# Longer allowances in a list scheduler's table: transfer to use, and VectorE or ScalarE to a matmul

## The chip, the cores and the metric

The kernel runs on one core of a Trainium2 chip. Its time is device microseconds, from the runs of the whole program; lower is better. The core's engines each take their instructions in the order in which they were issued: TensorE (PE, with its weight loads PEld), VectorE (DVE), ScalarE (ACT), GpSimd (POOL), and SyncE (SP), which here issues all DMA transfers.

## The reference, cut to what matters

Two layers over 1024 tokens of width 1024. In each, a normed and modulated input goes through one wide projection, whose columns feed three branches; their gated outputs are joined, projected back and added to the input. A last norm ends it. Everything is fp32.

```python
for l in range(DEPTH):                                    # DEPTH = 2
    mod = c_act @ ada_w[l] + ada_b[l]
    shift, scale, gate = jnp.split(mod[:, None, :], 3, axis=-1)
    h = rms_norm(x, norm_w[l]) * (1.0 + scale) + shift
    (q_lat, kv_lat, k_pe, g_mla, z, xbc, dt_raw,
     r, k, v, w_lo, a_lo, g_rwkv) = split_cols(h @ w_in[l], IN_SPLIT_SIZES)
    y_mla = mla_branch(...) * jax.nn.silu(g_mla)          # chunk-causal attention, 4 heads
    y_ssd = ssd_branch(...)                               # state space, chunks of 64
    y_rwkv = rwkv7_branch(...) * jax.nn.silu(g_rwkv)      # delta-rule recurrence, 8 heads of 64
    x = x + gate * (jnp.concatenate([y_mla, y_ssd, y_rwkv], axis=-1) @ w_out[l])
return rms_norm(x, final_norm_w)
```

## The kernel before, in words

The tokens are taken in two halves of 512, so there are four stages i = 0 to 3 (layer 0 half 0, layer 0 half 1, layer 1 half 0, layer 1 half 1). Each stage has two parts.

- **dense(i)**: the wide projection. 37 output tiles of 128 columns, each 24 matmuls of 128x512 into one PSUM bank of the tag `mf` (two banks in all). A weight tile comes in by DMA as `wr`, is split into a high part `wh` (ScalarE) and a low part `wl` (VectorE), and multiplies the split input (`h` tiles): high by high, high by low, low by high, in the type fp32r. ScalarE copies a finished bank to a tile `ct`, which SP stores to DRAM as `U`. From stage 2 on, dense(i) begins with the output projection of the layer before (`outproj`, 288 matmuls). After stage 3 come two more output projections (one for each half); the last of them ends with `outproj_last`, 48 matmuls over the last rwkv pair and the last attention head.
- **consumers(i)**: the branches. `rwkv` takes four pairs of heads in turn: `rwkv_a1` and `rwkv_a2` prepare them, `rwkv_bx` transposes through one PSUM bank of the tag `ra` (`ps623` to `ps633` are its banks for pair 1 of stage 0), `tinv_a` solves a triangular system in small VectorE steps, `rwkv_mr` and `chain` run the recurrence over eight chunks. In `chain`, each chunk's matmuls (`bx` by `gg`, 128x64) need the state that ScalarE and VectorE made of the chunk before. `ssd` and `mla` follow at the next rank; the attention of a head ends in a matmul with `vs` into `ps` (`ps4617` in the very last one), which VectorE multiplies into `gt`; SP stores it to `yd`, from where `y_split` loads it (`ct`), and ScalarE and VectorE split it into `h` tiles for `outproj`.

None of these calls issues an instruction. They are recorded as `Op`s, and `Plan.order` then writes one order for all engines: a list scheduler that steps through modelled time. For each queue (S is ScalarE, V VectorE, G GpSimd, P TensorE, Q SyncE) it keeps the ops whose inputs are there at the modelled time, and takes the one of the best rank. Ranks come from `plan.ahead`: rwkv before ssd and mla, these before the dense matmuls, so that the dense matmuls fill TensorE when no branch is ready; weight loads, weight splits and bank copies rank ahead of all. The order is fixed when the program is built: on the chip an engine does not skip an instruction that waits.

The table `LATENCY` enters at every edge between two ops. A key is the producer's letter and the consumer's: `SP` is ScalarE to TensorE, `VP` VectorE to TensorE, `D` stands for a DMA on either side. It is added to the producer's modelled end when the consumer becomes ready, and it is also added in `seat` when a buffer or a PSUM bank is taken over from its last user:

```python
t = max([t] + [end + LATENCY[at + o.at] for at, (end, _) in slots[tag][0][1].items()])   # seat: a freed buffer
ready[j] = max(ready[j], end + LATENCY[o.at + ops[j].at])                                # order: an input
```

All instructions are recorded on one line, L396, where the ordered ops are issued; the profile is therefore read by tile names.

Of the kernel before, what the change touches and what calls it, by code (L numbers as in the profile page):

```python
# [55 lines left out]
SG = ()  # L56
# [14 lines left out]
SX, SV, SB = 0, 0, 0  # L71
# [15 lines left out]

LATENCY = {"SS": 143, "SD": 147, "SV": 142, "SP": 270, "SG": 170, "VS": 128, "VD": 122, "VV": 127, "VP": 256, "VG": 155,  # L90
           "PS": 197, "PV": 196, "PD": 220, "PG": 224, "PP": 3, "GS": 75, "GD": 67, "GV": 60, "GP": 135, "GG": 102,
           "DS": 1700, "DV": 1700, "DP": 1850, "DG": 1700, "DD": 1700}


DMA_SP = True
# [148 lines left out]
class Plan:  # L244
# [41 lines left out]
    def order(self):  # L286
# [12 lines left out]
        def seat(o):  # L299
            t = 0.0  # L300
            for name in o.tiles:
                x = tiles[name]
                if x["free"] is None:
                    tag = x["tag"]
                    n = len(slots[tag]) - (0 if name.startswith("leafl") else owed[tag])
                    if n <= name.startswith("leafh") or not name.startswith("leaf") and name not in line[tag][:n]:
                        parked[tag].append(o)
                        return None
                    t = max([t] + [end + LATENCY[at + o.at] for at, (end, _) in slots[tag][0][1].items()])
                else:  # L310
                    t = max([t] + [end + LATENCY[at + o.at] for at, (end, _) in x["free"].items()])
                if x["bank"]:
                    t = max([t] + [end + LATENCY[at + o.at] for at, (end, _) in x["ends"].items() if at != o.at])
            return t
# [10 lines left out]
        while turn < len(ops):  # L325
# [58 lines left out]
            for j in o.next:  # L384
                ready[j] = max(ready[j], end + LATENCY[o.at + ops[j].at])
                wait[j] -= 1
# [1367 lines left out]
```

## Time and profile before

| | |
|---|---|
| median of 3 runs | 1990.66 us (1990.63 to 1992.5) |
| profiled execution: its time | 1993.3 us |
| profiled execution: first to last instruction | 1991.4 us |
| TensorE (PE) busy | 1848.3 us, 93% |
| VectorE busy | 1615.6 us, 81% |
| ScalarE busy | 1211.8 us, 61% |
| DMA packets, share of the 16 engines | 58.5% |
| mean granted TensorE clock | 0.972 |

Times in the profile are microseconds from the span's first instruction; the time of the profiled execution is 1.9 us above its span and 2.6 us above the median. TensorE's busy time comes from matmuls whose ends are modelled and which overlap, so the idle time between them and the granted clock say more than the share.

### The profile page before, as it was taken

How to read it: one execution, taken by the hardware profiler on the slowest of the kernel's cores; microseconds unless marked ns; L12 is line 12 of the kernel's file. 1: busy time of each engine (PE TensorE's matmuls, PEld its weight loads, DVE VectorE, ACT ScalarE, POOL GpSimd, SP SyncE). 2: the span in 40 equal slices, each digit the busy share in tenths (PEclk: the TensorE clock that was granted, in tenths of full speed). 3: DMA queues.
4: the chain of work that ended last, by engine and by line, in shares of the span. 5: the costliest groups of instructions: out<-in, count | busy, mean ns of one | idle time of the engine just before them, and what ended most of it. 6: DMA issues, size and time to landing. Idle time of an engine off the chain costs nothing. (4 is left out here: it accounts for less than half of the span.)

```text
span 1991.4 us, 32320 instructions
## 1 busy us (share of the span) xinstructions
PE 1848.3 (93%) x10220; PEld 1450.4 (73%) x10220; DVE 1615.6 (81%) x4002; ACT 1211.8 (61%) x2520; POOL 202.9 (10%) x302
## 2 busy tenths in 40 slices
PE   5899978999999996999999999999999999999997
PEld 3677756777777774777787777787777877777775
DVE  7798886888987898887678887878787888778766
ACT  6555565666555665746656647666656657676653
POOL 2100010001010101011100010002011010000101
PEclk9999988999999997999999999999999999999998
DMA  7676655755666576753555475855457556663542
GB/s 243 212 192 172 184 169 151 216 159 171 182 155 178 162 218 185 239 160 119 159 141 161 136 209 164 253 157 159 119 150 169 146 172 183 204 200 104 167 145 93
DMA packets 273371, 341.31 MB, mean 171 GB/s; under 512 B 79153, under 2 KB 132017, under 8 KB 273201
## 3 DMA queue, kind: packets, MB, share of 16 engines
q1 hardware_dynamic: 273200, 339.25, 58.5%
q8 instruction: 81, 1.33, 0.3%
q14 instruction: 90, 0.73, 0.1%
HBM read 254.67 MB, written 84.47 MB: 170 GB/s over the span
## 5 line engine op out<-in xcount | busy, mean ns | idle before, releaser
L396 PE MATMUL ps<-h,wh 128*128 128x512 f32 x3136 | 1021.1, 409 | 41.7 <-ACT ct L396 23.3
L396 PEld LDWEIGHTS ps<-h,wh 128*128 128x128 f32 x3136 | 580.8, 191 | 179.9 <-ACT ct L396 36.1
L396 PE MATMUL ps<-h,wl 128*128 128x512 f32 x1568 | 590.2, 408 | 2.3 <-DVE wl L396 2.3
L396 PE MATMUL ps<-b,b 128*128 128x128 f32 (+4 forms) x1512 | 388.9, 359 | 11.8 <-ACT b L396 4.0
L396 ACT ACTIVATE wh<-wr 128x512 fp32r<-128x512 f32 (+1 forms) x398 | 245.6, 620 | 220.1 <-PE ps L396 178.4
L396 PEld LDWEIGHTS ps<-h,wl 128*128 128x128 f32 x1568 | 296.8, 191 | 61.5 <-issue 4.8
L396 DVE TENSOR_TENSOR wl<-wr,wh 128x512 fp32r<-128x512 f32 (+1 forms) x398 | 268.7, 680 | 81.6 <-ACT wh L396 64.0
L396 PEld LDWEIGHTS ps<-b,b 128*128 128x128 f32 (+1 forms) x1512 | 232.2, 183 | 75.5 <-ACT b L396 18.1
L396 ACT ACTIVATE b<-b 128x512 f32<-128x512 f32 (+3 forms) x222 | 137.3, 626 | 71.6 <-DVE b L396 24.8
L396 DVE TENSOR_TENSOR b<-b,b 128x512 fp32r<-128x512 f32 (+4 forms) x178 | 121.4, 688 | 33.1 <-ACT b L396 32.2
L396 ACT ACTIVATE b<-ps 128x512 f32<-128x512 f32 (+3 forms) x201 | 99.5, 509 | 68.2 <-PE ps L396 63.0
L396 DVE TENSOR_TENSOR tmp<-Q,rq 128x60 f32<-128x60 f32 (+24 forms) x496 | 106.6, 215 | 5.7
L396 DVE TENSOR_TENSOR rq<-rq,tmp 128x60 f32<-128x60 f32 (+24 forms) x496 | 105.6, 213 | 5.2
L396 PEld LDWEIGHTS ps<-bx,gg 128*128 128x128 f32 x512 | 77.6, 194 | 41.3 <-ACT bx L396 14.4
L396 ACT ACTIVATE ct<-ps 128x512 f32<-128x512 f32 x150 | 88.1, 590 | 29.5 <-DMA U<-ct 9.9
L396 PE MATMUL ps<-cst,b 128*128 128x128 f32 x452 | 81.6, 282 | 15.2 <-POOL b L396 14.8
L396 POOL COPY halo<-ct 128x3 f32<-128x3 f32 x84 | 32.7, 389 | 616.2 <-ACT ct L396 616.1
L396 PE MATMUL ps<-bx,gg 128*128 128x64 f32 x512 | 83.5, 273 | 12.6 <-ACT bx L396 7.1
L396 ACT ACTIVATE b<-ps,s,s 128x512 f32<-128x512 f32 (+2 forms) x96 | 64.1, 669 | 39.3 <-DVE s L396 33.6
L396 PEld LDWEIGHTS ps<-cst,b 128*128 128x128 f32 x452 | 58.8, 146 | 30.9 <-POOL b L396 14.8
L396 DVE SCALAR_TENSOR_TENSOR h<-ps,md,h 128x512 f32<-128x512 f32 x72 | 53.7, 748 | 26.6 <-PE ps L396 26.1
L396 PEld LDWEIGHTS ps<-gg,bk 128*128 128x128 f32 x512 | 65.0, 193 | 14.1 <-issue 5.9
(196 smaller groups left out, 2598.7 us busy)
## 6 DMA issues: line engine op xcount, KB each, us to landing
wr<-in_w_in_dram SPq DMA_DIRECT2D x282, 256.0 KB
U<-ct SPq DMA_DIRECT2D x84, 257.5 KB
wr<-in_w_out_dram SPq DMA_DIRECT2D x80, 256.0 KB
U<-ct SPq DMA_DIRECT2D x64, 256.0 KB
ct<-in_ada_dram SPq DMA_DIRECT2D x64, 256.0 KB
ri<-U SPq DMA_DIRECT2D x52, 257.5 KB
b<-accd SPq DMA_DIRECT2D x96, 128.0 KB
ct<-yd SPq DMA_DIRECT2D x48, 256.0 KB
```

Source lines behind the costliest of these rows:

```text
L396: o.fn(*o.args, **o.kw)
```

## The change

Seven entries of the table grow; no op is added or removed, and each engine has the same instructions as before.

```diff
-LATENCY = {"SS": 143, "SD": 147, "SV": 142, "SP": 270, "SG": 170, "VS": 128, "VD": 122, "VV": 127, "VP": 256, "VG": 155,
+LATENCY = {"SS": 143, "SD": 147, "SV": 142, "SP": 500, "SG": 170, "VS": 128, "VD": 122, "VV": 127, "VP": 500, "VG": 155,
            "PS": 197, "PV": 196, "PD": 220, "PG": 224, "PP": 3, "GS": 75, "GD": 67, "GV": 60, "GP": 135, "GG": 102,
-           "DS": 1700, "DV": 1700, "DP": 1850, "DG": 1700, "DD": 1700}
+           "DS": 2200, "DV": 2200, "DP": 2350, "DG": 2200, "DD": 2200}
```

ScalarE to TensorE gets 230 ns more, VectorE to TensorE 244 ns more, and a transfer to whatever uses its data or its buffer 500 ns more. The scheduler thus sees a matmul ready later after its ScalarE or VectorE producer, and puts other ready matmuls ahead of it. In program order, the last matmul of dense(0) moves from place 1419 to 1196 among TensorE's 8408 matmuls and transposes, that of dense(1) from 3019 to 2863; the last chunk of the rwkv recurrence moves from 2102 to 2301 in stage 0, and from 3806 to 3989 in stage 1. In stages 2 and 3 these four kinds of places differ by less than 60.

Three places in the order matter below. Rows are an instruction's output tile, its inputs, its output's size and, after an x, how many follow each other.

**Place 1, TensorE, `rwkv_bx` of pair 1 in stage 0.** `ps410`, `ps439` and `ps448` are banks of dense(0); `ps617` is the bank of a head sum just ahead of the transposes `ps623` and on. Before:

```order
L396 MATMUL ps410_517<-h2153_260,wl416_523 128x512
L396 MATMUL ps617_724<-leafh618_725,bones_r_107 2x512
L396 MATMUL ps617_724<-leafl619_726,bones_r_107 2x512
L396 MATMUL ps623_730<-cst_99,gg565_672 128x128 x4
L396 MATMUL ps624_731<-cst_99,gg565_672 128x128 x4
L396 MATMUL ps625_732<-cst_99,bk564_671 128x128 x4
L396 MATMUL ps626_733<-cst_99,bk564_671 128x128 x4
L396 MATMUL ps862_969<-cst_99,b2859_966 128x128 x4
L396 MATMUL ps628_735<-cst_99,rv543_650 128x128 x4
L396 MATMUL ps633_740<-gg630_737,bk629_736 128x128 x4
```

Now:

```order
L396 MATMUL ps617_724<-leafl619_726,bones_r_107 2x512
L396 MATMUL ps439_546<-h2128_235,wl445_552 128x512
L396 MATMUL ps448_555<-h262_169,wh450_557 128x512
L396 MATMUL ps439_546<-h2141_248,wh444_551 128x512
L396 MATMUL ps448_555<-h263_170,wh450_557 128x512
L396 MATMUL ps439_546<-h2142_249,wh444_551 128x512
L396 MATMUL ps448_555<-h262_169,wl451_558 128x512
L396 MATMUL ps623_730<-cst_99,gg565_672 128x128 x4
```

Before, the transposes stand one bank behind the other, and 17 rows stand between `ps410` and the next dense row (`ps420`); now dense rows stand between all of them.

**Place 2, TensorE, `chain` of pair 1 in stage 1, near the start of dense(2).** `ps1710` takes the recurrence's first four chunks; `ps1510` and `ps1519` are banks of dense(1). Before:

```order
L396 MATMUL ps1710_1817<-bx1680_1787,gg1618_1725 128x64
L396 MATMUL ps1510_1617<-h21145_1252,wh1512_1619 128x512
L396 MATMUL ps1510_1617<-h21144_1251,wl1513_1620 128x512
L396 MATMUL ps1510_1617<-h21146_1253,wh1512_1619 128x512
L396 MATMUL ps1510_1617<-h21147_1254,wh1512_1619 128x512
L396 MATMUL ps1510_1617<-h21146_1253,wl1513_1620 128x512
L396 MATMUL ps1510_1617<-h21148_1255,wh1515_1622 128x512
```

Now:

```order
L396 MATMUL ps1707_1814<-bx1619_1726,Ez0_102 128x128 x4
L396 MATMUL ps1729_1836<-wa1547_1654,lora490_597 128x512
L396 MATMUL ps1729_1836<-wa1548_1655,lora490_597 128x512
L396 MATMUL ps1708_1815<-bx1619_1726,Ez0_102 128x128 x4
L396 MATMUL ps1915_2022<-cst_99,b21912_2019 128x128 x4
L396 MATMUL ps1710_1817<-bx1680_1787,gg1618_1725 128x64 x5
L396 MATMUL ps1921_2028<-cst_99,b21919_2026 128x128 x4
L396 MATMUL ps1710_1817<-bx1680_1787,gg1618_1725 128x64 x3
L396 MATMUL ps1922_2029<-cst_99,s1920_2027 128x128 x4
L396 MATMUL ps1711_1818<-bx1680_1787,gg1618_1725 128x64 x2
```

Here it goes the other way: dense(1) is already used up, and the chunks of `chain` now stand one behind the other with no dense row between them.

**Place 3, SP, the last attention output.** `gt4614` is that output, `yd3917` its place in DRAM, `ct4931` its way back into `y_split`; the `wr` loads are weights of the last output projection. Before:

```order
L396 DMA yd3917_4024<-gt4614_4721 128x256
L396 DMA wr4904_5011<-in_w_out_dram 128x384
L396 DMA ct4931_5038<-yd3917_4024 128x512
L396 DMA wr4908_5015<-in_w_out_dram 128x384
L396 DMA wr4912_5019<-in_w_out_dram 128x384
L396 DMA wr4916_5023<-in_w_out_dram 128x384
L396 DMA wr4920_5027<-in_w_out_dram 128x384
L396 DMA wr4924_5031<-in_w_out_dram 128x384
L396 DMA wr4934_5041<-in_w_out_dram 128x2x128 x2
```

Now:

```order
L396 DMA wr4924_5031<-in_w_out_dram 128x384
L396 DMA wr4934_5041<-in_w_out_dram 128x2x128 x2
L396 DMA wr4939_5046<-in_w_out_dram 128x2x128 x2
L396 DMA wr4944_5051<-in_w_out_dram 128x2x128 x2
L396 DMA wr4949_5056<-in_w_out_dram 128x2x128 x2
L396 DMA yd3917_4024<-gt4614_4721 128x256
L396 DMA ct4931_5038<-yd3917_4024 128x512
L396 DMA out_0_dram<-h24801_4908 128x512
```

The store and the load back moved behind all weight loads. On TensorE, the last attention matmul (into `ps4617`) was followed by 108 matmuls of the output projection before the first that reads the split of `ct4931` (`h24932`); now 16 stand between the two.

## The prediction

> **What bounds the kernel now.** I read the page's table of engines first, then the clock by slices, the waits of TensorE (PE), the windows in which it idles, and last the timeline of the end.
>
> ```profile
> PE 1848.3 (93%) x10220; PEld 1450.4 (73%) x10220; DVE 1615.6 (81%) x4002; ACT 1211.8 (61%) x2520; POOL 202.9 (10%) x302
> PE   5899978999999996999999999999999999999997
> PEclk9999988999999997999999999999999999999998
> core 0: 1991.4 us, clock 0.972
> ```
>
> PE is busy 93% and the bound over most of the span; the slices where it is not (first, sixth, sixteenth, last) are also those where the clock drops. VectorE (DVE) is busy 81%, so it can become the bound for a stretch of tens of us. No instruction is added, so the change can only alter PE's idle time and its clock. That idle time, by what ended it:
>
> ```profile
> PE ps L396 <- ACT ct L396: 23.3, 14, 3.6
> PE ps L396 <- POOL b L396: 14.8, 1, 14.8
> PE ps L396 <- ACT h L396: 10.6, 10, 1.9
> PE ps L396 <- ACT bx L396: 9.4, 10, 3.7
> PE ps L396 <- DVE ac L396: 9.1, 1, 9.1
> PE ps L396 <- DVE bx L396: 7.1, 5, 1.9
> PE ps L396 <- DVE h L396: 5.4, 10, 1.2
> PE ps L396 <- ACT gg L396: 5.1, 9, 2.3
> PE ps L396 <- ACT b L396: 4.0, 10, 0.9
> PE ps L396 <- DVE b L396: 3.8, 5, 1.4
> PE ps L396 <- DMA b<-accd: 3.7, 1, 3.7
> ACT b L396 <- DMA b<-accd: 17.2, 9, 6.0
> ```
>
> The columns are us in total, times, longest. The 14.8 us for POOL is the start of the program, which no allowance shortens. PE waits for a DMA itself only once, 3.7 us; so the 500 ns more on transfers acts on PE only through what ACT and DVE do later. The eight rows on ACT (ct, h, bx, gg, b) and on DVE (bx, h, b) make 68.7 us in 73 waits, 0.94 us each. That is four times the 0.23 us that an edge gains: most of these waits come from a producer whose queue is late, and not from the hop that the table prices.
>
> Three places carry the sum. The first is the transposes of pair 1 in stage 0 (Place 1), here in windows of us, each engine's busy time and count, the clock, the share of DMA and its GB/s, and then in PE's timeline and ACT's waits in the first window:
>
> ```profile
> 285.00:316.00 31.00, 14.28 (x49) 9.65 (x50) 25.78 (x75) 15.80 (x31) 3.87 (x5) 0.59 0.24 75
> 316.00:322.00 6.00, 6.00 (x16) 4.70 (x17) 3.40 (x5) 0.97 (x2) 0.19 (x1) 0.55 0.77 215
> ...
> 288.71 1.11 PE L396 MATMUL ps<-cst,gg 128*128 128x128 f32 x4 [0.68 <-ACT rt L396]
> 295.69 1.12 PE L396 MATMUL ps<-cst,bk 128*128 128x128 f32 x4 [2.26 <-ACT gg L396]
> 298.45 1.12 PE L396 MATMUL ps<-cst,rv 128*128 128x128 f32 x4 [0.79 <-ACT gg L396]
> 308.62 1.11 PE L396 MATMUL ps<-cst,s 128*128 128x128 f32 x4 [3.87 <-POOL s L396]
> 315.82 1.22 PE L396 MATMUL ps<-h,wh 128*128 128x512 f32 x2 [2.56 <-ACT ct L396]
> 318.54 0.63 PE L396 MATMUL ps<-h,wh 128*128 128x512 f32 x1
> 318.97 0.63 PE L396 MATMUL ps<-b,b 128*128 128x512 f32 x1
> 321.71 0.40 PE L396 MATMUL ps<-h,wh 128*128 128x512 f32 x1
> 321.95 0.39 PE L396 MATMUL ps<-b,b 128*128 128x512 f32 x1
> ...
> ACT b L396 <- DVE b L396: 7.7, 2, 7.4
> ```
>
> In 31 us PE works 14.28 and idles 16.7, while DVE is busy 25.78. Each transpose waits for the step before it, no dense row stands between, and the next dense row waits in its turn for ACT's copy of a bank (`ct`), which ACT reaches late because it has stood 7.4 us on DVE. The clock is 0.59 and stays 0.55 for 6 us after: dense matmuls there start 0.43 us apart (318.54 to 318.97), and 0.24 us apart once it is back (321.71 to 321.95). Of the 20.3 us busy in both windows, at a mean clock of 0.58, full speed would have saved some 8 (20.3 x 0.42 = 8.5). So this one place costs 16.7 + 8, about 25 us.
>
> The second is the boundary between dense(1) and dense(2):
>
> ```profile
> 757.00:779.00 22.00, 9.78 (x27) 6.80 (x28) 20.16 (x59) 7.06 (x12) 4.13 (x5) 0.53 0.75 252
> 779.00:790.00 11.00, 7.53 (x31) 5.05 (x30) 8.05 (x14) 9.61 (x15) 0.00 (x0) 1.00 0.32 81
> 766.71 1.11 PE L396 MATMUL ps<-cst,ac 128*128 128x128 f32 x4 [9.14 <-DVE ac L396]
> ```
>
> DVE is busy 20.16 of 22 us, so it is the bound there; PE idles 12.2 and 3.5 us and runs its 9.78 at 0.53, some 20 us lost in all (12.2 + 3.5 + 9.78 x 0.47 = 20.3).
>
> The Trainium skill has a rule on this ("TensorE: Matmul & The Clock Gate", section "What's actually happening"): TensorE drops to half clock after an idle window of about 3.4 us and needs about as long busy to come back. The trace agrees, with 0.53 around a wait of 9.14 us.
>
> The third is the end, from the last attention matmul to the use of its split (Place 3; SPq is the issue on SP's queue):
>
> ```profile
> 1938.95 0.39 PE L396 MATMUL ps<-b,b 128*128 128x128 f32 x2
> 1939.92 0.38 SPq L396 DMA_DIRECT2D yd<-gt  x1
> 1943.52 0.42 SPq L396 DMA_DIRECT2D ct<-yd  x1
> 1944.27 18.62 SPq L396 DMA_DIRECT2D wr<-in_w_out_dram  x13
> 1947.34 0.62 ACT L396 ACTIVATE h<-ct 128x512 fp32r<-128x512 f32 x1
> 1948.62 1.29 DVE L396 SCALAR_TENSOR_TENSOR h<-ct,h 128x512 fp32r<-128x512 f32 x2
> 1964.31 0.39 PE L396 MATMUL ps<-h,wh 128*128 128x512 f32 x1
> 1964.77 0.62 PE L396 MATMUL ps<-h,wh 128*128 128x512 f32 x2
> ...
> 1950.00:1964.00 14.00, 14.00 (x62) 10.73 (x61) 8.56 (x14) 3.72 (x7) 0.00 (x0) 1.00 0.37 107
> ```
>
> The way round DRAM takes from 1939.34 to 1949.91, 10.6 us; PE computes the output projection meanwhile without a gap and needs the split only at 1964.77.
>
> **The change, term by term.**
>
> *Place 1, a gain.* In the new order dense rows stand between all transposes of this stretch, so the waits of 0.68 to 3.87 us have matmuls to fill them and the clock has no reason to fall. DVE's 25.78 us of work remain; they lie beside dense work instead of beside nothing. At best the whole 25 us go; at worst none, if dense rows themselves wait for ACT's copies behind the 7.4 us on DVE. I take -25: in the new order three and more dense rows, on two banks, stand between one transpose and the next.
>
> *What pays for it.* The matmuls used there are not there later: dense(0) and dense(1) end 223 and 156 places earlier, the recurrences of stages 0 and 1 180 to 200 places later. Hence Place 2: ten groups of `chain` matmuls (5, 3 and 2 in the rows shown) without a dense row between, each needing the state that ACT and DVE make of the one before. The trace of before has no such hop uncovered; the nearest rows are the uncovered transposes at 288.71 and 298.45, with 0.68 and 0.79 us for one hop. Ten of them make 7 us. The low end is 0 (branch matmuls between may cover them); the high end doubles a hop, since the state passes through two engines: 14. I take +7.
>
> *The boundary.* DVE's 20.16 busy us in 22 do not depend on where dense matmuls stand, and what is late there, `ac`, is DVE's own queue. I take it as unchanged, 0; it could lose half its 20 us if the new order brings DVE's work forward, or gain as much if still less dense work is left for it.
>
> *Place 3, a loss.* Of 108 rows between the last attention matmul and the first that needs its split, 16 are left: 16 x 0.23 = 3.7 us of cover (0.23 is 1964.31 to 1964.77 over two rows). The chain is 10.6 us as it was. A part of it, the 3.6 us from store to load, holds for the new order too, since the load needs the store's data; with one split of the two needed first the chain is 7 to 8.6 us (to ACT's end, 1947.96). The hole is then 3.3 (7 - 3.7) to 6.9 us (10.6 - 3.7). Behind it stand some 42 matmuls of 0.23, 10 us; if the clock falls, part of them runs at half speed, by the row of 0.55 over 6 us above 2.7 us more (6 x 0.45). I take 5 for the hole and 2 for the clock, +7, between 3 and 10. By the skill's rule above, a hole under 3.4 us leaves the clock alone and one of 5 to 7 can halve it; the sum would be 1972 with the clock kept and 1974 with it halved.
>
> *SP's queue.* The store and the load back now stand behind all 14 remaining `wr` loads. Before, 13 of these were issued from 1944.27 on over 18.62 us, 1.4 us each, as the splits released their buffers. In the new order the last attention matmul itself stands 92 rows (108 - 16), some 21 us, later among the projection's matmuls, so the loads have that time and are out when it ends: 0. Should some be late, each adds 1.4 us to the hole; three would use up its high end.
>
> *The ordinary waits.* Outside those places, an edge allowed 0.23 us more can shorten a wait by at most that: 73 x 0.23 = 17 us. Since the mean wait is four times the allowance, and what is late is the queue, I take a third, -6 (0 to -17).
>
> *The transfers.* The 17.2 us that ACT waits for `accd` in 9 waits fall by at most 9 x 0.5 = 4.5 us, on ACT, 61% busy; behind ACT stands a DVE or PE step that has other work. Taken as 0.
>
> Sum: 1991.4 - 25 + 7 + 7 - 6 = 1974.4 for the span. The profiled execution's time lies 1.9 above its span and 2.6 above the median of the three runs, so the median becomes 1974.4 + 1.9 - 2.6 = 1973.7. I forecast 1974 us, 0.8% faster; its own range, with the term ends -25 to -15, 0 to 14, 3 to 10 and -17 to 0, is about 1958 to 1990 (not all ends at once).
>
> **Rivals.**
>
> *Slower: DVE is the bound through all of stages 0 and 1, and PE's idle time only moves.* For it speaks DVE's 25.78 of 31 and 20.16 of 22 us in both holes: PE waits where DVE is full, and dense work spent early is missing at the next such place. Then the 25 us of Place 1 return at the boundary or at the chains (the dense matmuls moved, 223 places x 0.23 = 51 us, are more than enough to open such a hole), and Place 2's clock falls as well. Time: 1991 + 7 for the tail, + 7 for Place 2, nothing else gained, 2004; 1998 to 2008. It decides once the early gain keeps less than the 14 us that the tail and Place 2 cost. Against it: outside the holes DVE has 19% idle, and PE is 93% busy without it.
>
> *No change.* The waits are set by late producers, allowances of 0.23 us reorder without filling, and Place 1's gain stops at some 14 us against the same costs: 1988 to 1994, about 1990. Against it stands that the new order visibly has dense rows in Place 1.
>
> *A larger gain.* The ordinary waits fall by their full 17 us, as dense rows step in wherever a producer is late, and the boundary's 20 us halve since DVE's queue reaches it earlier: 1974 - 11 - 10 = 1953. For it: ACT's `ct`, the largest row (23.3 us), is a wait for a bank and so a scheduled edge. Against it: the longest waits are producers that are full, which no order of PE makes faster.
>
> **Chances.** Main forecast 0.50, larger gain 0.16, no change 0.11, slower 0.23. 0.2%, 4 us, is about what a measurement of this kernel can tell from no change; so faster 0.66, the same 0.11, slower 0.23. The range 1945 to 2006 takes in the larger gain's time with 8 us below it and the slower rival's 2004.
>
> **What would show it.** Place 1 right: around the transposes of pair 1 in stage 0, PE is 95% busy or more and the clock stays at 1.00; wrong: a window with the clock near 0.6 there, or PE waiting on `ct` for several us. Place 2 right: a dozen waits of 0.5 to 1 us on `bx` ahead of `chain`'s matmuls at the start of dense(2), no more than 14 us together; wrong: a window of 20 us and more with the clock near 0.5. Place 3 right: one wait of 3 to 7 us for `h` in the last 30 us, some 42 matmuls before the last; wrong: no such wait. The ordinary waits right: the same eight rows at some 60 us; at 50 or less the larger gain has happened. The prediction fails as a whole if the boundary's loss, which I left as it is, grows by more than 15 us, which a wait on DVE longer than 9.14 us with a second half-clock stretch beside it would show.

## The result, and the profile after

The changed kernel takes 1955.28 us (median, 1952.39 to 1962.57) beside 1991.18 for the kernel before: a ratio of 0.9825 with an interval of 0.9811 to 0.984, 36 us faster where 17 were forecast. The profiled execution has a span of 1951.8 us, 39.6 less than before: the two profiled executions lie some 4 us further apart than the medians (1953.6 and 1993.3 us). Its table of engines, slices and clock:

```profile
PE 1825.9 (94%) x10220; PEld 1460.7 (75%) x10220; DVE 1619.7 (83%) x4002; ACT 1205.9 (62%) x2520; POOL 204.4 (10%) x302
PE   5899997999999986989999999998999999999996
PEclk9999998999999986999999999999999999999997
core 0: 1951.8 us, clock 0.975
```

The weak sixth slice of before is strong now, the seventh (293 to 342 us) has become weak in its place, and slices 15 and 16, 683 to 781 us, show 8 and 6, where before had 9 and 6. PE's waits by releaser (us in total, times, longest):

```profile
PE ps L396 <- ACT h L396: 21.4, 13, 3.4
PE ps L396 <- DVE b L396: 11.2, 9, 3.3
PE ps L396 <- DVE bx L396: 9.0, 7, 2.2
PE ps L396 <- DVE h L396: 7.7, 11, 1.5
PE ps L396 <- ACT ct L396: 5.4, 8, 2.6
PE ps L396 <- ACT bx L396: 3.8, 5, 1.7
PE ps L396 <- ACT b L396: 3.5, 7, 0.8
PE ps L396 <- ACT gg L396: 3.0, 7, 1.4
```

The eight rows that made 68.7 us in 73 waits make 65.0 in 67. Read as a total they say that next to nothing happened. Over all rows on ACT and DVE PE's waits fall from 103.7 us in 116 waits to 87.1 in 94, and they have moved in time, which the windows tell. The program is cut below where PE has done 600 and 900 us of the same matmul work in both kernels (how that is counted follows); first the three windows of before, then of the change, with PE busy, PEld, DVE, ACT, POOL, clock, DMA share and GB/s:

```profile
15.00:732.00 717.00, 654.63 (x3599) 504.05 (x3599) 608.73 (x1539) 433.13 (x910) 68.66 (x117) 0.96 0.64 182
732.00:1073.00 341.00, 317.50 (x1687) 250.50 (x1686) 277.62 (x705) 207.33 (x423) 34.50 (x50) 0.96 0.56 166
1073.00:1974.00 901.00, 872.77 (x4924) 693.68 (x4923) 715.62 (x1734) 559.07 (x1165) 84.90 (x116) 0.99 0.56 164
```

```profile
15.00:683.00 668.00, 630.09 (x3492) 500.10 (x3492) 588.04 (x1491) 418.11 (x885) 70.93 (x120) 0.99 0.68 196
683.00:1051.00 368.00, 329.49 (x1797) 261.30 (x1795) 300.86 (x742) 222.57 (x454) 35.73 (x52) 0.93 0.53 154
1051.00:1934.00 883.00, 862.95 (x4920) 697.27 (x4920) 717.02 (x1747) 553.17 (x1158) 82.83 (x112) 0.99 0.57 167
```

The first part is 49 us shorter (idle 62.4 to 37.9, clock 0.96 to 0.99), the middle, which holds the boundary from dense(1) to dense(2), 27 us longer (clock 0.96 to 0.93), the last 18 us shorter.

For the finer picture each matmul is given the median distance to the next start that its tiles and shape have in the trace of before; the running sum is PE's work, 1740 us in every kernel, and time less work is what has been lost so far. The table is that loss, as a difference to the kernel before (whose time at each mark stands in the first row), from the profiled execution of each kernel. The rows below the first two belong to the experiments.

| PE work done, us | 180 | 240 | 300 | 480 | 600 | 720 | 900 | 1320 | 1680 | 1737 |
|---|---|---|---|---|---|---|---|---|---|---|
| before: time | 239 | 333 | 400 | 603 | 732 | 883 | 1073 | 1531 | 1914 | 1974 |
| the change | -12.6 | -42.1 | -31.9 | -49.5 | -49.3 | -28.9 | -22.7 | -34.5 | -46.0 | -39.8 |
| hops 500 alone | +2.6 | -11.3 | -12.0 | -22.9 | -24.8 | -29.1 | -25.4 | -34.9 | -33.2 | -34.8 |
| hops 380 alone | +4.1 | -25.5 | -23.2 | -36.8 | -13.6 | +8.9 | +6.4 | -0.8 | -3.9 | -6.2 |
| hops 250 alone | +5.8 | -6.7 | -7.8 | -19.2 | +3.0 | +0.5 | +6.7 | +10.3 | +1.1 | +3.4 |
| hops 800 with transfers | -3.7 | -31.5 | -25.5 | -44.7 | -28.4 | -38.8 | -40.6 | -52.8 | -53.8 | -31.3 |
| the change in stage 0 only | -13.3 | -44.5 | -33.1 | -48.5 | -27.3 | -0.6 | +0.1 | +1.9 | +4.6 | +3.0 |
| the change with hops 480 | -9.2 | -35.4 | -25.6 | -41.8 | -27.7 | -3.1 | -2.4 | -5.4 | -5.1 | -7.0 |
| old table from stage 3's branches on | -12.3 | -43.9 | -33.0 | -50.8 | -50.0 | -29.6 | -23.7 | -30.8 | -32.5 | -33.3 |
| old table in stage 3's attention | -12.9 | -44.4 | -34.4 | -52.2 | -52.7 | -32.2 | -25.5 | -34.4 | -41.6 | -44.4 |

Of the change's 39.8 us, 17.3 are less idle time of PE, 3.3 are less time lost to the clock (half of the busy time at a granted clock of 0.5), and 19.2 are less time counted as busy at full clock. The wait lists show the first of these three alone.

**Place 1.** The transposes of pair 1 in stage 0 in the changed kernel, two windows and PE's timeline (the bracket is the idle time ahead and what ended it):

```profile
274.00:304.00 30.00, 29.22 (x143) 23.53 (x142) 27.66 (x77) 19.63 (x40) 8.48 (x9) 1.00 0.63 190
304.00:330.00 26.00, 17.22 (x63) 12.67 (x62) 23.93 (x50) 14.30 (x23) 3.01 (x5) 0.80 0.62 195
...
293.56 0.60 PE L396 MATMUL ps<-cst,bk 128*128 128x128 f32 x4
301.15 1.13 PE L396 MATMUL ps<-gg,bk 128*128 128x128 f32 x8 [0.78 <-issue]
312.28 0.50 PE L396 MATMUL ps<-h,wh 128*128 128x512 f32 x1 [3.42 <-ACT h L396]
323.30 1.11 PE L396 MATMUL ps<-cst,b 128*128 128x128 f32 x4 [3.31 <-DVE b L396]
```

PE is busy 29.22 of 30 us at full clock, beside DVE's 27.66. Right behind it, dense(0) is used up and dense(1) waits for its split input `h`: 8.8 us idle in the second window, and a clock of 0.80.

**Place 2 and the boundary.** Three windows, and in the second the waits of `chain`'s matmuls, the longest wait of another branch and the first dense row (the sixth wait of `chain`, 0.40 us, stands in the last section):

```profile
676.00:692.00 16.00, 8.93 (x52) 6.95 (x53) 13.53 (x39) 7.76 (x18) 0.00 (x0) 0.81 0.80 226
730.00:764.00 34.00, 21.36 (x89) 16.48 (x89) 30.89 (x86) 18.64 (x34) 4.37 (x4) 0.71 0.37 116
764.00:796.00 32.00, 22.33 (x89) 15.26 (x89) 28.93 (x77) 18.83 (x37) 4.11 (x3) 0.83 0.42 130
...
738.78 1.12 PE L396 MATMUL ps<-bx,gg 128*128 128x64 f32 x4 [2.16 <-DVE bx L396]
743.84 0.69 PE L396 MATMUL ps<-bx,gg 128*128 128x64 f32 x2 [1.82 <-DVE bx L396]
747.20 1.12 PE L396 MATMUL ps<-cst,s 128*128 128x128 f32 x4 [2.67 <-POOL s L396]
748.82 1.20 PE L396 MATMUL ps<-h,wh 128*128 128x512 f32 x2
755.22 0.44 PE L396 MATMUL ps<-bx,gg 128*128 128x64 f32 x2 [0.42 <-DVE bx L396]
757.12 0.43 PE L396 MATMUL ps<-bx,gg 128*128 128x64 f32 x2 [1.46 <-DVE bx L396]
759.16 0.69 PE L396 MATMUL ps<-bx,gg 128*128 128x64 f32 x2 [1.60 <-DVE bx L396]
```

The second window loses 12.6 us idle and, at a clock of 0.71 on 21.36 busy us, 6 more. Six of its waits, of 0.40 to 2.16 us and 7.9 us together, are the chain's own on `bx`, five of them ended by DVE, which is busy 30.89 of the 34 us. The other 4.7 us idle are waits of the branches beside it, 2.67 us on POOL's `s` the longest. Only up to 748.82 is the chain without dense rows; from there on rows of the output projection stand between its matmuls again.

**Place 3.** The end, SP's queue, ACT and PE:

```profile
1896.83 18.21 SPq L396 DMA_DIRECT2D wr<-in_w_out_dram  x11
1915.09 0.59 SPq L396 DMA_DIRECT2D yd<-gt  x1
1917.70 0.33 SPq L396 DMA_DIRECT2D ct<-yd  x1
1920.33 0.63 ACT L396 ACTIVATE h<-ct 128x512 fp32r<-128x512 f32 x1 [3.24 <-DMA ct<-yd]
...
1917.71 0.73 PE L396 MATMUL ps<-h,wh 128*128 128x512 f32 x2 [0.62 <-DVE h L396]
1921.01 1.95 PE L396 MATMUL ps<-h,wh 128*128 128x512 f32 x4 [2.33 <-ACT h L396]
1924.23 1.22 PE L396 MATMUL ps<-h,wh 128*128 128x512 f32 x2 [0.42 <-DVE h L396]
```

The last weight load is issued until 1915.04 and the store at 1915.09, half a microsecond after `gt` was ready (1914.58), so the queue that the store was moved behind cost at most that, where nothing was forecast. The split comes after PE has run out: 3.4 us idle (0.62 + 2.33 + 0.42), and matmuls at half rate behind it (4 in 1.95 us). By equal work the change loses 6.2 us here (-46.0 to -39.8).

### The profile page after: what moved, and what is told of

It reads as the page before. It is cut to its first block, busy times and chain, and to the rows that moved or that the text cites. A ratio compares the mean times of both kernels' runs of the same rounds, so it can differ in the third digit from the quotient of the medians.

```text
span 1951.8 us, 32300 instructions
## 1 busy us (share of the span) xinstructions
PE 1825.9 (94%) x10220; PEld 1460.7 (75%) x10220; DVE 1619.7 (83%) x4002; ACT 1205.9 (62%) x2520; POOL 204.4 (10%) x302
## 5 line engine op out<-in xcount | busy, mean ns | idle before, releaser
L396 PE MATMUL ps<-b,b 128*128 128x512 f32 (+4 forms) x1512 | 384.6, 356 | 10.5 <-DVE b L396 6.3
L396 ACT ACTIVATE b<-b 128x512 f32<-128x512 f32 (+3 forms) x222 | 136.9, 625 | 62.1 <-DVE b L396 25.6
L396 PEld LDWEIGHTS ps<-bx,gg 128*128 128x128 f32 x512 | 76.8, 194 | 32.2 <-DVE bx L396 15.8
L396 POOL COPY halo<-ct 128x3 f32<-128x3 f32 x84 | 28.6, 340 | 621.9 <-ACT ct L396 594.2
L396 POOL TENSOR_TENSOR s<-s,nhalf 128x4 f32<-128x4 f32 (+1 forms) x34 | 54.0, 1591 | 258.1 <-DVE s L396 250.5
L396 DVE SCALAR_TENSOR_TENSOR h<-ps,md,h 128x512 f32<-128x512 f32 x72 | 53.5, 746 | 33.2 <-PE ps L396 32.7
L396 ACT ACTIVATE b<-ps,s,s 128x512 f32<-128x512 f32 (+2 forms) x96 | 63.9, 667 | 27.3 <-DVE s L396 24.3
```

Of the source, the lines that this page charges most:

```text
L396: o.fn(*o.args, **o.kw)
```

## The experiments

Each was timed against the kernel before on the same chip; the ratio and its interval are given. The chips differ from group to group, so kernels of different groups are compared by their ratios.

**Which entries carry it.** Two kernels change one part of the table, a third all of it by a tenth, and a fourth goes further.

```diff
+"SP": 500, "VP": 500                                # hops only
```


> Only ScalarE and VectorE to TensorE are raised to 500; the transfer entries stay as before. Theory A (the allowance for the hop puts ready matmuls ahead of each waiting one, so the ordinary waits shrink): nearly all of the gain is here, 1955 to 1965 us, and PE's waits for ACT's copies (ct, 23.3 us before) are at 10 us or less. Theory B (any change of the table reshuffles the order, and where clusters of unfilled waits fall is luck): anywhere from 1950 to 2005, no relation to what was raised. Theory C (the transfer entries carry it): 1985 to 1995.

1958.68 us, 0.9861 (0.984 to 0.9883): inside theory A's range, though PE's waits on `ct` fell to 13.2 us and not to 10.

```diff
+"DS": 2200, "DV": 2200, "DP": 2350, "DG": 2200, "DD": 2200   # transfers only
```


> Only the transfer entries are raised by 500; the hops to TensorE stay as before. Theory A: no gain from fewer waits, 1985 to 1995; the waits on ct stay at some 20 us. Theory B: anywhere from 1950 to 2005. Theory C: 1955 to 1965.

1990.39 us, 1.0017 (0.9999 to 1.0035): the transfers alone bring nothing. PE's waits on `ct` nevertheless fell, to 12.3 us in 15, so the expectation on `ct` was wrong: that row does not measure the gain.

```diff
+"SP": 293, "VP": 280, "DS": 1750, "DV": 1750, "DP": 1900, "DG": 1750, "DD": 1750
```


> Every entry is raised by a tenth of the change (293, 280, and 50 more for a transfer). The order is reshuffled, the allowance hardly differs. Theory A: a tenth of the gain, 1984 to 1991. Theory B: as far from before as the full change, 10 to 40 us either way. Theory C: as A.

1992.86 us, 1.003 (1.0019 to 1.0042): no gain, and 6 us slower than before on that chip (1986.79), which none of the three theories gave.

```diff
+"SP": 800, "VP": 800, "DS": 2200, "DV": 2200, "DP": 2350, "DG": 2200, "DD": 2200
```


> The hops to TensorE go to 800, the transfers as in the change. Theory A: the ordinary waits shrink further, but dense(0) and dense(1) are used up earlier still, and the boundary to dense(2) loses more: 1945 to 1965, with the waits outside 650 to 800 us under half of before. Theory B: no relation, 1950 to 2005.

1970.39 us, 0.9914 (0.988 to 0.9948). In the table it is 53.8 us ahead at 1680 and loses 22.5 at the end, where a single row is left between the last attention matmul and the use of its split. It misses theory A's range and its condition (outside 650 to 800 us PE waits 80.8 us on ACT and DVE, before 82.8). The transfers alone bring nothing so far; that the size of the hop decides does not follow, since theory B allows all of these times but that of the tenth.

**Inputs or buffers.** The hop enters at an input and where a bank or buffer is taken over; here only one of the two is raised.

```diff
+EDGE = dict(LATENCY, **{'SP': 500, 'VP': 500})
-                ready[j] = max(ready[j], end + LATENCY[o.at + ops[j].at])
+                ready[j] = max(ready[j], end + EDGE[o.at + ops[j].at])
```


> Hops of 500 only where a matmul's input comes from ScalarE or VectorE; taking over a bank or buffer keeps the old allowance, and so do the transfers. Theory A1 (PE's waits are for inputs of the branches, which now have dense rows ahead of them): most of the 28 us of the run with both uses, 1958 to 1968. Theory A2 (the gain is in the turnover of the dense banks, PE's waits on ct): 1980 to 1992, with ct at 20 us or more.

1980.88 us, 0.9965 (0.9948 to 0.9982).

```diff
+SEAT = dict(LATENCY, **{'SP': 500, 'VP': 500})      # for LATENCY in seat, three times
```


> The other half: hops of 500 only where a bank or buffer is taken over. Theory A1: 1980 to 1992. Theory A2: 1958 to 1968, with PE's waits on ct under 15 us.

1991.81 us, 1.0006 (0.9991 to 1.002). Together the two gave 28 us, apart 9 and nothing. Neither theory predicted that; the spread of the runs around 500 below is as large, so which use matters stays open.

**The tail, and 800 without it.** Operations recorded from stage 3's branches on are ordered by the old table.

```diff
+        plan.late = i == 3; consumers(i, U)         # late: LATENCY as before, else the change's table
```


> The changed kernel, but everything recorded from the branches of stage 3 on is ordered by the old table. Stages 0 to 2 have the order of the change, and 173 rows stand again between the last attention matmul and the first use of its split. If the tail's hole costs what the prediction said, 7 us (6 by the changed kernel's waits), its waits there go, and the time is 1948 to 1952 unless stage 3's own waits return (before had 10 us more there than the change): then 1952 to 1960.

1959.14 us, 0.9855 (0.9836 to 0.9874). Up to 900 us of work it runs like the change, and at 1320 it is 3.7 us behind it. The tail's loss is gone (-32.5 to -33.3), and from 1320 to 1680 it gains 1.7 where the change gains 11.5: with the same stages ahead of it, this part is 10 us slower by the old table. Both terms came out as expected.

> Hops of 800 in stages 0 to 2, transfers as before, the old table from the branches of stage 3 on; 155 rows of cover at the end. The run with 800 everywhere was 54 us ahead of before by equal PE work until the tail, and lost 22 there with one row of cover. Theory A: without that loss 1930 to 1950. Theory B (the order is luck, 800 no better than 500): 1950 to 1990.

The same switch with hops of 800 and the old transfers: 1970.89 us, 0.9907 (0.9875 to 0.9939). The tail's loss is gone too, but so are 33 us of the gain ahead of it (-20.8 at 1680). This contradicts theory A in its simple form. The transfers' entries differ as well between the two runs with 800, so the switch is not the only difference.

**The size.** Hops alone, with 77 rows or more of cover at the end.

```diff
+"SP": 100, "VP": 90
```


> The other direction: hops to TensorE of 100 and 90 instead of 270 and 256, transfers as before, 139 rows of cover at the end. Theory A (the allowance itself sets the waits): slower, 1995 to 2020, with more PE waits on ACT and DVE than the 73 of before. Theory B (the order is luck): 1960 to 2000 with no more waits.

2030.85 us, 1.0209 (1.0185 to 1.0234), 43 us slower; over all its rows PE waits 130 times on ACT and DVE, 119.8 us, beside 116 times and 103.7 us in the kernel before. The direction is theory A's; the loss is larger than its range.

```diff
+"SP": 380, "VP": 380
```


> Hops of 380, about half of the way, transfers as before; 97 rows of cover at the end (94 at 500). Theory A: between before and the 1958.7 of 500, 1965 to 1982. Theory B: unrelated, 1950 to 2000.

1988.37 us, 1.0004 (0.9991 to 1.0018), a miss for theory A. At 480 us of work it is 36.8 us ahead, at 720 it is 8.9 behind.

```diff
+"SP": 650, "VP": 650
```


> Hops of 650, transfers as before; 77 rows of cover at the end. Theory A, with dense matmuls that run out: 1950 to 1968, near 500. Theory B: unrelated, 1950 to 2000.

1975.18 us, 0.9928 (0.9903 to 0.9952), outside of what A gave as well.

**Does stage 0's gain last?**

```diff
+        plan.late = i > 0; U = dense(i, spread)
+        plan.late = i > 0; consumers(i, U)
```


> The change's table for everything recorded for stage 0 (dense(0) and its branches), the old one for the rest. By equal PE work the change was 49.5 us ahead of before at 480 us of work, gave 23 back at the boundary to dense(2), and won 19.5 in stages 2 and 3. Theory of the prediction (what dense work stage 0 uses early is missing at the boundary, whatever orders stage 1): 15 to 30 of the 49 are given back there, 1960 to 1980 in all. Rival (the boundary's loss comes from stage 1's own longer allowances): it keeps more than 40 of the 49, 1945 to 1955.

1991.39 us, 1.0013 (0.9991 to 1.0035). It is 48.5 us ahead at 480 us of work, as the change is, and level with before at 720: everything was given back, more than either theory said, 21 us of it between 480 and 600 us of work (until 705 us in this run) and 27 between 600 and 720 (until 882). Three of its windows there, and then the last of them in the change, where PE is busy without a gap:

```profile
650.00:700.00 50.00, 38.28 (x176) 30.05 (x175) 40.06 (x105) 29.81 (x65) 9.27 (x11) 0.92 0.60 188
750.00:800.00 50.00, 35.39 (x164) 25.97 (x164) 45.89 (x120) 24.05 (x47) 7.37 (x6) 0.88 0.28 93
800.00:850.00 50.00, 35.28 (x231) 28.46 (x229) 39.12 (x69) 26.76 (x51) 5.74 (x5) 0.72 0.54 163
```

```profile
800.00:850.00 50.00, 50.00 (x325) 42.37 (x324) 36.54 (x72) 28.62 (x60) 5.05 (x5) 1.00 0.71 222
```

So the loss does not need stage 1's own longer allowances, as the rival had it. But it is not bound to the change's stage 0 either: hops of 250 are 19.2 us ahead at 480 and 0.5 behind at 720, while hops of 500 alone go from 22.9 ahead to 29.1. An early gain is often given back there, not always, and what decides it is open.

**The size or the one order?** Three orders close to 500.

```diff
+"SP": 490, "VP": 490
```


> Hops of 490 instead of 500, transfers as before; 103 rows of cover at the end (94 at 500). If the size of the allowance decides: within 6 us of 500's 1958.7, 1952 to 1965. If the particular order decides: as far off as 380 and 650 are, 1965 to 1990.

1980.31 us, 0.9958 (0.9943 to 0.9973).

```diff
+"SP": 510, "VP": 510
```


> Hops of 510, transfers as before; only 22 rows of cover at the end, which costs some 5 us by itself. If the size decides: 1955 to 1970. If the order decides: 1950 to 1990, and by equal PE work before the tail more than 10 us away from 500.

1976.67 us, 0.9947 (0.9928 to 0.9966).

```diff
+"SP": 480, "VP": 480, "DS": 2200, "DV": 2200, "DP": 2350, "DG": 2200, "DD": 2200
```


> The change with hops of 480 instead of 500, transfers raised by 500 as in it; 116 rows of cover at the end. If the size decides: 1945 to 1960 (the change less its tail hole). If the order decides: 1960 to 1990.

1986.25 us, 0.9988 (0.997 to 1.0006). All three fell where the theory of the order put them (510 is also 13.1 us away from 500 by equal PE work at 1680). The last one fills Place 1 as the change does and is 41.8 us ahead at 480, then meets such a cluster one stage later, at the transposes of pair 2 of stage 1, and is 2.4 ahead at 900:

```profile
783.00:818.00 35.00, 14.57 (x54) 9.71 (x54) 32.13 (x77) 16.99 (x32) 4.91 (x5) 0.55 0.36 108
...
784.00 0.59 PE L396 MATMUL ps<-leafh,bones_r 128*2 128x512 f32 x1 [9.67 <-ACT leafh L396]
788.01 1.11 PE L396 MATMUL ps<-cst,gg 128*128 128x128 f32 x4 [0.69 <-ACT gt L396]
811.85 1.11 PE L396 MATMUL ps<-cst,s 128*128 128x128 f32 x4 [3.41 <-POOL s L396]
```

It is the picture of Place 1 before (14.28 busy of 31 us, DVE 25.78, clock 0.59), with PE idle and DVE full.

Two orders close to the old table, for their spread:

```diff
+"SP": 250, "VP": 236
```


> Hops of 250 and 236, transfers as before, 173 rows of cover at the end. If the size has a share (the five orders near 500 average 1972): these stay at 1980 to 2005, as before, the transfers alone and the tenth did (1987 to 1993). If it is all the order: as likely below 1980 as above.

1996.41 us, 1.0045 (1.0031 to 1.0059).

```diff
+"SP": 290, "VP": 276
```


> Hops of 290 and 276, transfers as before, 90 rows of cover at the end. As for 250: 1980 to 2005 if the size has a share, as likely below 1980 as above if it is all the order.

1983.92 us, 0.9973 (0.9949 to 0.9996).

So there are five orders with hops of 250 to 293 (before, transfers alone, the tenth, 250, 290) and five with 480 to 510 (the change, 500 alone, 490, 510, 480). The first have a mean ratio of 1.0013, from 0.9973 to 1.0045; the second one of 0.9916, from 0.9825 to 0.9988. Four of the second five lie below all of the first. So the size of the allowance is worth about 0.97%, some 19 us, in the mean; with five orders each that is rough (a 95% interval of some 0.1 to 1.8%). The order that comes out of it by chance moves the time by some 14 us near 500 (standard deviation of the five ratios, 0.0069) and by some 6 near the old table (0.0028). The other sizes fit: hops of 100 are slower than all (1.0209), 380 lie with the old table (1.0004), and 650 and 800 (0.9928, 0.9914, 0.9907) gain no more than the mean near 500. The change is the best of its five, 18 us below their mean.

**The tail by itself.** The change, with the old table for the attention of stage 3 alone:

```diff
+            plan.late = i == 3; mla(l, d, U, hf, m, yd); plan.late = False
```


> The change, but the attention of stage 3 alone is ordered by the old table; 161 rows stand between the last attention matmul and the use of its split. Stages 0 to 2 are as in the change. The tail's waits go (6 us) and the recurrence of stage 3 keeps its longer hops: 1944 to 1953. If stage 3's waits come back as with the old table for all of its branches: 1955 to 1962.

1947.52 us, 0.9796 (0.978 to 0.9812), inside the expected range. By the ratios it is 5.8 us below the change, whose interval (0.9811 to 0.984) its own just touches. From 1680 us of work on it gains 2.8 us where the change loses 6.2; ahead of that it is 4.4 us behind the change. In the stretch ahead of the end PE has no gap left:

```profile
1900.00:1922.00 22.00, 22.00 (x99) 18.15 (x98) 15.91 (x26) 7.68 (x14) 0.00 (x0) 1.00 0.35 100
```

## Why the prediction was right or wrong

The direction was right; the size was half of what came, 17 us against 36. Two steps failed: the price of the ordinary waits, and the zero for the boundary. By equal PE work, from one column of the table to the next, with the measured time split into PE's idle time, the loss to the clock, and the time counted as busy at full clock:

| term | forecast | measured | idle | clock | busy |
|---|---|---|---|---|---|
| Place 1 (180 to 300 us of work) | -25 | -19.3 | -10.5 | -4.1 | -4.7 |
| Place 2 and the boundary (600 to 900) | +7 and 0 | +26.6 | +15.0 | +9.6 | +2.0 |
| Place 3 (1680 to the end) | +7 | +6.2 | +3.0 | +3.2 | 0.0 |
| ordinary waits (the rest) | -6 | -53.3 | -24.8 | -12.0 | -16.5 |
| sum | -17 | -39.8 | -17.3 | -3.3 | -19.2 |

*Place 1* did what was said: PE 97% busy, full clock, 29.5 us gained from 180 to 240 us of work (-12.6 to -42.1). The 10 us back by 300, the end of dense(0), were not in the term.

*Place 2* came out near in its hops, by luck. Ten uncovered hops of 0.7 us were forecast, 7 us; the chain shows six, of 1.3 us in the mean, 7.9 us. The ten matmuls without a dense row are five chunks of two, so the count was too high, and the price, from a stretch in which one engine stood between two matmuls, too low. What the term left out is the clock, 6 us in these 34 us.

*The boundary* at 0 failed. Beside the hops some 19 us are lost from 600 to 900 us of work, 13 if the 6 of clock are put to Place 2: about the 15 that the prediction named as its failure as a whole, towards the end of 20 that I had named and not taken. The wait on DVE of over 9.14 us that was to show it did not come: from 683 to 1051 us the longest is 3.5, and the loss is spread over many waits and the clock. That less dense work was left for it (dense(1) ends 156 places earlier) fits, and so does the run with the change in stage 0 only; but hops of 500 alone lose nothing there, so this cause is in part argued.

*The tail* is the one term that came out nearly whole: hole 5 forecast, 3.4 measured; clock 2 forecast, about 2.8 (6.2 - 3.4). In both experiments that took the hole out, the loss after 1680 us of work is gone.

*The ordinary waits* are the step that failed most, -6 forecast and -53.3 measured. The term counted the listed waits alone: "An edge allowed 0.23 us more can shorten a wait by at most that", 17 us in all. Idle time outside the named places fell by 24.8 us, so that bound did not hold; it took the order as fixed with each row shifted by one matmul, and what the plan puts between producer and consumer is a whole other order. In the last part, stages 2 and 3, the change has 24 waits on ACT and DVE, 17.1 us, and before has 39, 26.1 us: a wait is still 0.7 us in the mean, but there are 15 fewer. The term also put nothing down for the clock, 12.0 us outside the named places, and nothing for the time counted as busy, 16.5 us; what makes up the latter is not shown. The experiment that gave stage 3 back to the old table shows 10 us in that stage alone. The sign that I had set for this term, the eight rows at some 60 us, came out at 65.0 and told nothing of it.

*The rivals.* The slower one was half right: idle time does move. With the change in stage 0 only, all 48.5 us came back, at the boundary and ahead of it and not from the tail, and with hops of 480 nearly all. In the change itself half of it stayed (-22.7 at 900). The larger gain's time of 1953 is near the measured one by luck: its ordinary waits gained more than its 17 us, but it had the boundary's loss halve, and the loss doubled.

Two slips in the prediction move nothing: the clock shows no drop in the first slice (9 tenths or more there), and the slower rival's sum is 2005, not 2004.

The gap of 19 us between forecast and result is close to what the change's order lies below the mean of its kind (18 us), and the forecast's 17 us to that mean. But the terms behind the 17 were not right one by one: too little gain and too little loss offset each other, so that nearness is luck as well. Why this order keeps half of its early gain past the boundary, and that of 480 none, is shown as to the place (the cluster at 783 to 818 us; in the change the transposes of that pair stand in the window from 764 to 796 us, with PE busy 22.33 of 32 us at a clock of 0.83) and stays open as to the cause.

## What to carry to other kernels

A table that feeds a list scheduler is judged over several neighbouring values and not by one: here 10 ns more or less than 500 moved the time by 17 to 19 us, as much as the allowance itself. A stretch filled with work taken from later can be a loan: follow it past the point where that work runs out (here the next stage boundary, with VectorE full) before it is counted as a gain. The list of waits misses time: here it shows 17 of 40 us, so count PE's progress by equal work as well. And the end of the program, the one place with nothing left to fill, was priced from the trace of before to about a microsecond, and its loss was taken out by itself.

## What the runs showed of the hardware

The granted clock can halve without a long wait. At Place 2 of the changed kernel the last matmuls at full rate start at 736.18, and the four at 738.78 take 1.12 us where four at 735.12 took 0.66; the wait between them is 2.16 us, and none since 720 is longer:

```profile
732.00:739.00 7.00, 3.08 (x19) 2.43 (x20) 6.83 (x16) 3.10 (x6) 0.00 (x0) 0.87 0.39 124
739.00:748.00 9.00, 4.26 (x18) 3.65 (x19) 8.03 (x30) 5.12 (x9) 2.48 (x2) 0.50 0.21 60
...
735.12 0.66 PE L396 MATMUL ps<-bx,gg 128*128 128x64 f32 x4
736.18 0.44 PE L396 MATMUL ps<-bx,gg 128*128 128x64 f32 x2 [0.40 <-ACT bx L396]
```

A clock of 0.87 over these 7 us is 1.8 us at half rate (0.13 x 7 / 0.5), so the drop came near 737.2, 0.6 us into that wait; of the 5.2 us before it PE was busy 2.9. The tail shows it too, half rate behind a wait of 2.33 us. The rule cited in the prediction (the Trainium skill, "TensorE: Matmul & The Clock Gate", "What's actually happening") speaks of an idle window of about 3.4 us; by these rows a stretch of short waits in which PE is busy about half of the time is enough, and the sentence that a hole under 3.4 us leaves the clock alone did not hold.
